# Gathering both experts' token columns in one transposed step, in a mixture-of-experts encoder layer

## The chip, the cores and the metric

The kernel runs on one core of a Trainium2 chip. Times are device microseconds (us) of one execution. The time shown for the kernel before is the median of three runs; one more execution was recorded with a profile, and all rows below come from it. PE is TensorE, DVE is VectorE, ACT is ScalarE, POOL is GpSimd, SP is the engine that issues the transfers (DMA).

## The reference, cut to what matters

One layer of an encoder over 256 tokens of 1024 features: three token mixers (attention, a state-space scan, a convolution), merged and projected, then a normalisation, then a mixture of experts with a second normalisation. What the change touches is the mixture of experts:

```python
logits = (t @ router_w + router_b)
top_vals, top_idx = lax.top_k(logits, 4)            # 4 of 32 experts for each of 256 tokens
gates = softmax(top_vals)
def expert_block(xe, e):                            # xe: the rows of t routed to expert e
    h = xe @ w_gu[e] + b_gu[e]                      # 1024 -> 2048
    gate, up = h[:, :1024], h[:, 1024:]
    gate = minimum(gate, 7.0); up = clip(up, -7.0, 7.0)
    return ((up + 1) * (gate * sigmoid(1.702 * gate))) @ w_dn[e] + b_dn[e]   # 1024 -> 1024
out[token] += gates * expert_block(t[token], e)
x = LN(2**0.25 * x + out)
```

An expert's weights are 12 MB in float32 (8 MB up, 4 MB down), so 32 experts are 384 blocks ("units") of 1 MB.

## The kernel before, in words

The first part of the program (up to L1031) computes the mixers with all weights streamed as 512 KB pieces and split into a rounded part and a remainder, so that each product runs as three products in the format fp32r. While it runs, SP also loads the first units of the experts' weights into a ring of 19 slots of 1 MB (`ring_tile`, L726, and `do_pre`, L732). Unit n uses the slot that unit n-19 had, so from then on SP can issue a load only when PE has used that earlier unit (`load`, L746, in the program's order).

The middle part (L1033 to L1110, a written-out order for all engines) finishes the first normalisation, computes the router's logits, picks the four experts of each token (`choose`), counts for each expert the place of each token (`ranks`), and builds for the first pair of experts a matrix of zeros and ones, `ohp`: one row for each token, one column for each of 64 slots of either expert (`onehot`). `gather_first` multiplies the normalised rows `nrm` (float32, which PE runs as two records for each product) by `ohp`: the result already has the features on the partitions and the slots as columns. `xcopy` applies the scale and shift of the normalisation while it copies PSUM to `xg0`. From `size` the program knows for each expert whether it has up to 32 tokens (0), 33 to 64 (1), or 65 to 96 (2). The rest of the middle part makes what later experts need: `nh_` and `nl_` (the rounded part and the remainder of `nrm`, by ACT at L1093 and by DVE at L939), the gates, and the accumulator `acc`, which POOL writes from `nrm` and the scaled row `lnt` (L1109, L1110).

Then the experts run one after the other (`expert`, L1224), in pairs that share one gather. PE follows the written order; ACT and DVE are ordered by the framework inside a block, and a runtime `If` ends a block. An expert of size 1 runs the arm of 64 columns (`up_many`, tile `pGL`), of size 0 the arm of 32 columns (`up_four`, tile `pGS`), of size 2 both. The 32 columns lie in a tile of their own, `xsm`:

- `small_columns` (L1015) copies the first 32 of the 64 columns with ACT;
- `small_onehot` (L1008) makes their zeros and ones with DVE;
- `If(both > 1)` (L1248) gathers, for an expert of size 2 alone, tokens 65 to 96 into `xsm`: 32 products of 32 columns and 8 copies.

`flush` adds the expert before to `acc`. `fill`, between the up and the down products, gathers for the next pair: in the even expert 8 products of 512 columns give rows of tokens (`gather`, L979), which ACT and DVE copy to `raw`; in the odd expert 8 transposes turn them (`spread_rows`, L994) and 8 copies write `xg`. Then come the down products (L1312 for 64 columns, L1343 for 32), after the transposes of the hidden values (`pTL`, `pTS`) that ACT copies to `hT` (L1306, L1329).

Tiles of the middle part lie in the pool `ch`, which is closed at L1111; the pool `ex` of the experts' temporaries is opened in its place, and each of its tiles waits for the tiles that lay there.

Of the kernel before, what the change touches and what calls it, by code (L numbers as in the profile page):

```python
# [30 lines left out]
TOP = CAP + TINY  # L31
LIMIT = 7.0
# [149 lines left out]
def tile_trunk(ctx, tc, xT_d, xn_d, wf_d, vec_d, row_d, rw_d, cst_d, cst2_d, rope_d, ln1_d, ln2_d,  # L182
# [697 lines left out]
    x1t = [mo.tile([P, KT, P], F32, tag="xg", name=f"x1t{c}", bufs=2) for c in range(2)]  # L880
    raw = mo.tile([P, D], F32, name="rawx")
    xgx = raw.rearrange("p (k n) -> p k n", k=KT)
# [8 lines left out]
    ohp = [mo.tile([P, 2, 2, CAP], F32R, tag="ohp", name=f"ohp{t}", bufs=2) for t in range(1)]  # L891
# [49 lines left out]
    def choose(c):  # L941
        lg = ch.tile([P, NE], F32, name=f"lg{c}")
# [25 lines left out]
    def gates(c):  # L968
        gq = ch.tile([P, 4, NE], F32, tag="gq", name=f"gq{c}", bufs=1)
        V.reciprocal(gs[c][:, 1:2], gs[c][:, 1:2])  # L970
        V.tensor_scalar_mul(ge[c], ge[c], gs[c][:, 1:2])
        V.tensor_tensor(gq, eq[c], ge[c].unsqueeze(2).to_broadcast([P, 4, NE]), op=ALU.mult)
        V.tensor_reduce(Gm[c], gq.rearrange("p k e -> p e k"), axis=AX.X, op=ALU.add)

    def onehot(dst, c, e0):
        V.tensor_tensor(dst[:, c], C("iota_s", 0, CAP).unsqueeze(1).to_broadcast([P, 2, CAP]),
                        rank[c][:, e0:e0 + 2].unsqueeze(2).to_broadcast([P, 2, CAP]), op=ALU.is_equal)

    def gather(pg, c, oh, parts=(0, 1)):  # L979

        for i in parts:
            src = (nh_, nl_)[i]
            for hf in range(2):
                T.matmul(pg[hf], oh, src[:, c, hf * 512:(hf + 1) * 512],
                         start=(c == 0 and i == 0), stop=(c == 1 and i == 1))

    def xcopy(dst, src, k):

        if k >= KT // 2:
# [4 lines left out]
    def spread_rows(dst, src, name):  # L994
        for hf in range(2):
            pT = sm(f"pgt{name}{hf}", [P, 4, P])
            for k in range(4):
                T.transpose(pT[:, k], src(4 * hf + k), C("ident"))
            for k in range(4):
                xcopy(dst[:, 4 * hf + k], pT[:, k], 4 * hf + k)  # L1000

    def gather_first(c):

        for k in range(KT):
            T.matmul(pgd[k // 4][:, k % 4], nrm[c][:, k * P:(k + 1) * P], pair(ohp[0], c).bitcast(F32),
                     start=(c == 0 and k % 4 == 0), stop=(c == 1 and k % 4 == 3))

    def small_onehot(e):  # L1008
        ohs = mo.tile([P, 2, TINY], F32R, tag="ohs", name=f"ohs{e}", bufs=2)
        for c in range(2):  # L1010
            V.tensor_scalar(ohs[:, c], C("iota_s", 0, TINY), base[:, e:e + 1], rank[c][:, e:e + 1],
                            op0=ALU.add, op1=ALU.is_equal)
        return ohs

    def small_columns(e, xg):  # L1015
        lo = (e % 2) * CAP
        xs_ = mo.tile([P, KT, TINY], F32, tag="xsm", name=f"xsm{e}", bufs=1)
        A.copy(xs_, xg[:, :, lo:lo + TINY])  # L1018
        return xs_

    def rowk(k):
        return raw[:, k * P:(k + 1) * P]

    def pair(oh, c):
        return oh[:, c].rearrange("p r s -> p (r s)")
# [5 lines left out]

    PO.memset(rankT.bitcast(F32), 0.0)
    with tc.manual_schedule():  # L1033
# [22 lines left out]
        nrm = [raw, ch.tile([P, D], F32, name="nrm")]  # L1056
# [8 lines left out]
        ranks(0)  # L1065
        zip_run(choose(1), [lambda: None, lambda: V.tensor_mul(rank[0], Pm[0], prk[0]),
# [10 lines left out]
        for c in range(2):  # L1077
# [5 lines left out]
        few = ch.tile([P, NE], F32, name="few")  # L1083
# [12 lines left out]
        for c in range(2):  # L1096
            gates(c)
        cmx = ch.tile([P, 1], F32, name="cmx")
# [117 lines left out]
    def grp(t, g):  # L1216
        return t[g * TINY:(g + 1) * TINY]
# [6 lines left out]
    def expert(e, oh, xg, bl, wt, prev, cur, fill):  # L1224


        pe, da, both = [nc.values_load(size[0:1, e:e + 1], engines=g, min_val=0, max_val=2,
                                       skip_runtime_bounds_check_because="a sum of two comparisons of a count")
                        for g in ((ENG.PE,), (ENG.Activation, ENG.DVE), (ENG.PE, ENG.Activation, ENG.DVE))]
        lo = (e % 2) * CAP  # L1230
        s_ = slice(lo, lo + CAP)
        _, sc, yh, yl = cur

        ohs, xs_ = first if e == 0 else (small_onehot(e), small_columns(e, xg))
        pg = bank(5, f"pgs{e}", [P, KT, TINY])

        def gather_more():
            for k in range(KT):
                for c in range(2):
                    for i, src in enumerate((nh_, nl_)):  # L1240
                        T.matmul(pg[:, k], src[:, c, k * P:(k + 1) * P], ohs[:, c],
                                 start=(c == 0 and i == 0), stop=(c == 1 and i == 1))

        def copy_more():
            for k in range(KT):
                xcopy(xs_[:, k], pg[:, k], k)

        with tc.If(both > 1):  # L1248
            gather_more()
            copy_more()  # L1250
# [13 lines left out]
        def up_four(k0):  # L1264
# [4 lines left out]
            for k in (k0, k0 + 1):  # L1269
                for g, (h, q) in enumerate(QUARTERS):  # L1270
                    T.matmul(grp(pS, g).rearrange("p (g n) -> p g n", g=2), xs_[:, k],  # L1271
                             quarter(wt[k], h, q), start=False, stop=(k == KT - 1))

        for k0 in range(0, KT, 2):
# [82 lines left out]
    def heavy_gather(e, part, ohx):  # L1357
        nm = f"{e}h{part}"
        pg = [sm(f"pgx{nm}{hf}") for hf in range(2)]
        for c in range(2):  # L1360
            gather(pg, c, ohx[:, c])
        rows = []
        for i in range(4):
            r = ex.tile([P, 256], F32, tag=("gv", "uv")[i % 2], name=f"raw{nm}{i}", bufs=2 + i % 2)
            (V.tensor_copy if i % 2 else A.copy)(r, pg[i // 2][:, i % 2 * 256:(i % 2 + 1) * 256])
            rows.append(r)
        spread_rows(xgx, lambda k: rows[k // 2][:, k % 2 * P:(k % 2 + 1) * P], nm)

    def heavy(e, part, wt, cur):
# [3 lines left out]
        heavy_gather(e, part, ohx)  # L1373
# [31 lines left out]
    ENG = mybir.EngineType  # L1405
# [201 lines left out]
```

## Time and profile before

| | us |
|---|---|
| median of three runs (1362.12 to 1366.07) | 1365.44 |
| the profiled execution's own time | 1365.53 |
| its span, first to last instruction | 1363.7 |
| PE busy, share of the span | 1140.3, 84% |
| DVE busy | 559.5, 41% |
| ACT busy | 330.2, 24% |
| moved from memory: 453.27 MB, mean over the span | 333 GB/s |

The span is the profiled execution; 1.83 us lie around it. In the rows, times are from the start of the span. A row of a timeline merges like instructions: start, duration of the merged stretch, engine, line, operation, tiles and shape, count, and in brackets the idle time of that engine before it and what ended it. The letter q behind an engine is its sequencer, which handles branches and semaphores. A float32 product stands as two records, an fp32r product as one; both are printed as f32.

### The profile page before, as it was taken

Reading aid. Unit: us, or ns where it says so; the run is one execution under the profiler, and the core shown is the slowest. Engines: PE = TensorE matmul, PEld = TensorE weight load, DVE = VectorE, ACT = ScalarE, POOL = GpSimd, SP = SyncE. Lnnn points to the kernel's source line nnn. Section 1 sums busy time; section 2 is a strip of 40 time slices with the busy share of each in tenths; the row PEclk is TensorE's granted clock in tenths of the full one; section 3 lists DMA queues with packets and bytes.
Section 4 is the critical chain, followed back from the end, with each engine's and each line's share of the span. In section 5 each row is a group of like instructions: output and inputs, shape, how many; then the busy total and the mean of one; then the engine's idle time right before and its main releaser. Section 6 shows DMA issues by size and latency. Waiting matters only on the chain. (4 is left out here: it accounts for less than half of the span.)

```text
span 1363.7 us, 21824 instructions
## 1 busy us (share of the span) xinstructions
PE 1140.3 (84%) x8035; PEld 595.8 (44%) x8035; DVE 559.5 (41%) x1206; ACT 330.2 (24%) x690; POOL 169.1 (12%) x93
## 2 busy tenths in 40 slices
PE   7999899989978987888888779898888688767875
PEld 6877789889833332322332223232322232212222
DVE  3668888866752323322332222322233222222214
ACT  5666665644421110110010111111111101000101
POOL 3442234457130000000000000000000000000000
PEclk9999899999988999999999899998999999988978
DMA  7334345468879899999999999998999999999991
GB/s 228 124 109 155 124 140 186 155 209 282 313 283 419 344 371 397 418 419 419 417 419 420 419 419 418 420 419 357 387 417 417 419 419 420 418 419 420 418 393 39
DMA packets 73627, 456.47 MB, mean 335 GB/s; under 512 B 8304, under 2 KB 8704, under 8 KB 26752
## 3 DMA queue, kind: packets, MB, share of 16 engines
q1 hardware_dynamic: 73472, 454.35, 83.2%
q8 instruction: 103, 1.69, 0.5%
q14 instruction: 52, 0.43, 0.1%
HBM read 453.27 MB, written 1.05 MB: 333 GB/s over the span
## 5 line engine op out<-in xcount | busy, mean ns | idle before, releaser
L1271 PE MATMUL pGS<-ew,xsm 128*32 128x512 f32 x1408 | 183.8, 627 | 57.4 <-DMA ew<-in_wgu_dram 33.2
L1261 PE MATMUL pGL<-ew,xg 128*64 128x512 f32 x832 | 198.2, 615 | 3.2 <-DMA ew<-in_wgu_dram 2.9
L1205 DVE TENSOR_TENSOR xn<-xn,pos 128x512 f32<-128x512 f32 x124 | 79.8, 684 | 218.1 <-PE pos L1201 218.1
L247 POOL TENSOR_TENSOR wl<-raw,wh 128x1024 fp32r<-128x1024 f32 x56 | 136.8, 2450 | 160.9 <-ACT wh L246 154.6
L1194 DVE SCALAR_TENSOR_TENSOR yl<-pY,gsl,yh 128x512 fp32r<-128x512 f32 x35 | 26.3, 751 | 244.1 <-ACTq L1248 103.3
L1134 ACT ACTIVATE sg<-gv 128x256 f32<-128x256 f32 x48 | 20.0, 417 | 437.5 <-DVE gv L1133 436.7
L1495 POOL TENSOR_TENSOR xn<-xn,lb 128x256 f32<-128x256 f32 x4 | 2.8, 728 | 959.8 <-DVE xn L1483 959.8
L1271 PEld LDWEIGHTS pGS<-ew,xsm 128*32 128x32 f32 x1408 | 44.2, 112 | 156.9 <-issue 93.8
L1343 PE MATMUL pY<-ew,hT 128*32 128x512 f32 x704 | 87.0, 628 | 24.6 <-ACT hT L1329 17.6
L1261 PEld LDWEIGHTS pGL<-ew,xg 128*64 128x64 f32 x832 | 57.4, 140 | 114.3 <-issue 93.5
L246 ACT CAST wh<-raw 128x1024 fp32r<-128x1024 f32 (+1 forms) x89 | 91.1, 1028 | 55.9 <-DMA raw<-in_wf_dram 17.3
L1312 PE MATMUL pY<-ew,hT 128*64 128x512 f32 x416 | 102.2, 648 | 0.0
L1193 ACT ACTIVATE yh<-pY,gsl 128x512 fp32r<-128x512 f32 x35 | 24.1, 687 | 197.0 <-PEq L1316 71.4
L247 DVE TENSOR_TENSOR wl<-raw,wh 128x1024 fp32r<-128x1024 f32 (+1 forms) x33 | 41.5, 1263 | 41.9 <-ACT wh L246 41.9
L1312 PEld LDWEIGHTS pY<-ew,hT 128*64 128x64 f32 x416 | 31.0, 149 | 61.9 <-issue 60.4
L1343 PEld LDWEIGHTS pY<-ew,hT 128*32 128x32 f32 x704 | 20.4, 114 | 75.6 <-issue 33.6
L1267 PE MATMUL pGS<-bgu_t,bl 128*32 128x512 f32 x176 | 26.3, 664 | 28.7 <-DVEq L1248 10.9
L1018 ACT COPY xsm<-xg 128x256 f32<-128x256 f32 x32 | 12.9, 402 | 148.4 <-PE pGS L1271 132.0
L1201 PEld LDWEIGHTS pos<-yh,sc 64*128 64x128 f32 x124 | 12.2, 183 | 56.9 <-issue 56.9
L1325 PE MATMUL pY<-bdn_t,bl 128*32 128x512 f32 x88 | 24.0, 623 | 14.3 <-PEq L1316 14.3
L1201 PE MATMUL pos<-yh,sc 64*128 64x512 f32 x124 | 31.0, 491 | 4.7 <-PEq L1277 4.7
L417 DVE SCALAR_TENSOR_TENSOR xacc<-xp,vec,xacc 128x256 f32<-128x256 f32 x48 | 32.4, 676 | 2.7 <-ACT xacc L415 1.5
(462 smaller groups left out, 2126.2 us busy)
## 6 DMA issues: line engine op xcount, KB each, us to landing
ew<-in_wgu_dram SPq DMA_DIRECT2D x241, 1024.0 KB, 19.9
ew<-in_wdn_dram SPq DMA_DIRECT2D x124, 1024.0 KB, 19.9
raw<-in_wf_dram SPq DMA_DIRECT2D x87, 512.0 KB, 3.6
ew<-in_wgu_dram SPq DMA_DIRECT2D x30, 512.0 KB, 6.3
ew<-in_wdn_dram SPq DMA_DIRECT2D x8, 512.0 KB, 4.6
xraw<-in_xT_dram SPq DMA_DIRECT2D x4, 256.0 KB, 5.8
xn<-in_xn_dram SPq DMA_DIRECT2D x2, 512.0 KB, 5.3
lnt<-in_ln_dram SPq DMA_DIRECT2D x2, 512.0 KB, 10.5
```

The costliest lines, as they stand in the source:

```text
L246: A.copy(h[:, b], raw[:, b])
L247: (PO if u in LOW_POOL else V).tensor_sub(l[:, b], raw[:, b], h[:, b].bitcast(F32))
L417: V.scalar_tensor_tensor(acc, xp[:, j:j + S], W("cw5", t * 5 + j), acc, op0=ALU.mult, op1=ALU.add)
L1193: A.activation(yh, pY, AF.Copy, scale=gsl)
L1194: V.scalar_tensor_tensor(yl, pY, gsl, yh.bitcast(F32), op0=ALU.mult, op1=ALU.subtract)
L1201: T.matmul(pos[n], sc[r, c * P:(c + 1) * P], y[r], start=(start and i == 0), stop=(i == 1))
L1205: V.tensor_add(dst, dst, po)
L1261: T.matmul(pL[q][h * 64:(h + 1) * 64].rearrange("p (g n) -> p g n", g=2), xg[:, k, s_], quarter(wt[k], h, q), start=False, stop=(k == KT - 1))
L1267: T.matmul(grp(pS, g), bl[:, g * TINY:(g + 1) * TINY].bitcast(F32), bgu_t[:, q * 512:(q + 1) * 512].bitcast(F32), start=True, stop=False)
L1271: T.matmul(grp(pS, g).rearrange("p (g n) -> p g n", g=2), xs_[:, k], quarter(wt[k], h, q), start=False, stop=(k == KT - 1))
L1312: T.matmul(pY[0][n * 64:(n + 1) * 64], hT[b][:, j, h * CAP:(h + 1) * CAP], wt[KT + 2 * b + h][:, j, n * 512:(n + 1) * 512], start=False, s ...
L1343: T.matmul(grp(pY, 2 * n + j), hT[:, j, g * TINY:(g + 1) * TINY], w[:, j, n * 512:(n + 1) * 512], start=(j == 1 and (b, h) == (0, 0)), sto ...
```

## The change

The two kinds of columns become one matrix. For a pair of experts `ohp` now has 192 columns: 64 and 64, then 32 and 32. `xg` holds 192 columns likewise, and `xsm`, `raw` and the copy L1018 are gone.

- `gather` now multiplies 128 features of `nh_` or `nl_` (the stationary operand) by the 192 columns of `ohp`: 4 products for each of 8 blocks of features. The even expert's `fill` gathers blocks 0 to 3, the odd expert's 4 to 7, each with four copies, two by ACT and two by DVE. The transposes are gone.
- For an expert of size 2 the 32 columns hold tokens 65 to 96, else the first 32 (through `base`), so the `If` of L1248 stands only for experts 0 and 1, whose small columns are still copied from the wide ones.
- In the middle part the first transpose of `prt` and a first half of the counts `pn` come ahead of the gather, the first gather runs by halves, the halves are copied by one engine each, and the small columns, the `If` and its register loads for expert 0 come ahead of the second transpose of `prt`, `rankT`, `nh_`, `lnt` and the gates. `nrm` has both its tiles in `ch`.

```diff
+SL = 2 * TOP
-    raw = mo.tile([P, D], F32, name="rawx")
-    ohp = [mo.tile([P, 2, 2, CAP], F32R, tag="ohp", name=f"ohp{t}", bufs=2) for t in range(1)]
+    ohp = [mo.tile([P, 2, SL], F32R, tag="ohp", name="ohp0", bufs=2)]
...
+    def onehot_small(dst, c, e):
+        V.tensor_scalar(small(dst, c, e), C("iota_s", 0, TINY), base[:, e:e + 1], rank[c][:, e:e + 1],
+                        op0=ALU.add, op1=ALU.is_equal)
+    def gather(dst, oh, k0, name):
+        n = oh.shape[-1]
+        pt = sm(f"pgx{name}{k0}", [P, 2, n])
+        for k in (k0, k0 + 1):
+            for c in range(2):
+                for i, src in enumerate((nh_, nl_)):
+                    T.matmul(pt[:, k - k0], src[:, c, k * P:(k + 1) * P], oh[:, c],
+                             start=(c == 0 and i == 0), stop=(c == 1 and i == 1))
+        for k in (k0, k0 + 1):
+            xcopy(dst(k), pt[:, k - k0], k, k // 2 % 2)
...
+    def more_columns(e, both, pg, rows):
+        with tc.If(both > 1):
+            ...
+            for k in range(KT):
+                xcopy(small(xg0, k, e), pg[:, k], k)
...
-        nrm = [raw, ch.tile([P, D], F32, name="nrm")]
+        nrm = [ch.tile([P, D], F32, name=f"nrm{c}") for c in range(2)]
...
         ranks(0)
+        pn = mm("pn", [P, NE])
+        T.matmul(pn, C("ones"), Pm[0], start=True, stop=False)
...
-        gather_first(0)
         T.transpose(prt[:, 0], rank[0], C("ident"))
+        gather_first(0, 0)
         ranks(1)
         V.tensor_mul(rank[1], Pm[1], prk[1])
         onehot(ohp[0], 1, 0)
-        pn = mm("pn", [P, NE])
-        for c in range(2):
-            T.matmul(pn, C("ones"), Pm[c], start=(c == 0), stop=(c == 1))
-        T.transpose(prt[:, 1], rank[1], C("ident"))
-        gather_first(1)
-        A.copy(rankT[0:NE], prt.rearrange("e c t -> e (c t)"))
+        T.matmul(pn, C("ones"), Pm[1], start=False, stop=True)
+        gather_first(0, 1)
...
+        for hf in range(2):
+            gather_first(1, hf)
+            for k in range(4):
+                xcopy(xg0[:, 4 * hf + k, 0:P], pgd[hf][:, k], 4 * hf + k, hf)
+        for e in range(2):
+            A.copy(xg0[:, :, P + e * TINY:P + (e + 1) * TINY], xg0[:, :, e * CAP:e * CAP + TINY])
+            if e == 0:
+                first = sizes(0)
+                more_columns(0, first[2], mm("pgs0", [P, KT, TINY]), (nrm,))
+        T.transpose(prt[:, 1], rank[1], C("ident"))
+        A.copy(rankT[0:NE], prt.rearrange("e c t -> e (c t)"))
...
-        ohs, xs_ = first if e == 0 else (small_onehot(e), small_columns(e, xg))
-        with tc.If(both > 1):
-            gather_more()
-            copy_more()
+        if e == 1:
+            more_columns(e, both, bank(5, f"pgs{e}", [P, KT, TINY]), ...)
...
-                    T.matmul(grp(pS, g).rearrange("p (g n) -> p g n", g=2), xs_[:, k],
+                    T.matmul(grp(pS, g).rearrange("p (g n) -> p g n", g=2), xg[:, k, x_],
...
                     for c in range(2):
                         onehot(ohn, c, e + 2)
+                        for i in range(2):
+                            onehot_small(ohn, c, e + 2 + i)
...
+        def fill(e=e, more=more):
+            if more:
+                for k0 in (0, 2) if e % 2 == 0 else (4, 6):
+                    gather(lambda k: xgn[:, k], ohn, k0, str(e))
```

The path for experts with more than 96 tokens uses the new `gather` too; with these inputs it is skipped.

## Rows read from the trace of the kernel before

**Rows 1.** Page, the span in 40 slices: busy tenths of the DMA engines.
```profile
DMA  7334345468879899999999999998999999999991
```
**Rows 2.** Windows: stretch, length, busy (count) by engine, clock, DMA share, GB/s.
```profile
378.00:394.00 16.00, 10.26 (x68) 4.40 (x72) 13.41 (x32) 6.07 (x10) 8.06 (x6) 0.85 0.35 133
469.00:481.00 12.00, 9.88 (x63) 3.13 (x60) 3.69 (x6) 1.61 (x3) 0.00 (x0) 1.00 0.35 132
509.00:515.00 6.00, 3.27 (x22) 0.93 (x22) 0.98 (x2) 0.69 (x1) 0.00 (x0) 1.00 0.43 147
514.00:930.00 416.00, 347.98 (x2312) 124.97 (x2306) 119.37 (x290) 48.37 (x114) 0.00 (x0) 0.95 1.01 419
930.00:942.00 12.00, 9.80 (x63) 2.98 (x59) 3.69 (x6) 1.42 (x3) 0.00 (x0) 1.00 0.60 237
970.00:974.00 4.00, 1.50 (x10) 0.37 (x10) 0.78 (x2) 0.69 (x1) 0.00 (x0) 0.93 0.44 127
```
**Rows 3.** Timeline of PE: the last wait for weights ahead of the late stops.
```profile
811.32 1.06 PE L1343 MATMUL pY<-ew,hT 128*32 128x512 f32 x8 [1.17 <-DMA ew<-in_wdn_dram]
```
**Rows 4.** Timeline of PE: last wait for weights, and the last expert's start.
```profile
1286.45 1.94 PE L1261 MATMUL pGL<-ew,xg 128*64 128x512 f32 x8 [0.29 <-DMA ew<-in_wgu_dram]
1312.68 1.19 PE L1257 MATMUL pGL<-bgu_t,bl 128*128 128x512 f32 x2 [6.95 <-DVEq L1444]
```
**Rows 5.** Timeline of PE: first and last of expert 2's 32 conditional products.
```profile
432.40 0.28 PE L1241 MATMUL pgs<-ohs,nh 128*128 128x32 f32 x1
435.88 0.26 PE L1241 MATMUL pgs<-ohs,nl 128*128 128x32 f32 x1
```
**Rows 6.** Windows, columns as above: a stretch of mixer products of 256 columns.
```profile
320.00:340.00 20.00, 20.00 (x171) 20.00 (x171) 14.11 (x21) 9.82 (x13) 13.74 (x6) 1.00 0.86 302
```
**Rows 7.** Timeline of PE: an even expert's gather, to its down products.
```profile
461.48 0.73 PE L984 MATMUL pgx<-nh,ohp 128*128 128x512 f32 x2
463.45 0.40 PE L1302 MATMUL pY<-bdn_t,bl 128*128 128x512 f32 x1
464.99 7.09 PE L1312 MATMUL pY<-ew,hT 128*64 128x512 f32 x32
```
**Rows 8.** Timeline of PE: experts 3 and 15, from their transposes to down products.
```profile
499.12 1.06 PE L998 MATMUL pgt<-cst,rawx 128*128 128x128 f32 x8
503.96 7.09 PE L1312 MATMUL pY<-ew,hT 128*64 128x512 f32 x32
...
843.31 1.09 PE L998 MATMUL pgt<-cst,rawx 128*128 128x128 f32 x8
848.32 9.86 PE L1312 MATMUL pY<-ew,hT 128*64 128x512 f32 x32
```
**Rows 9.** Timeline, all engines: first gather to first expert's transposes.
```profile
378.39 2.47 PE L1005 MATMUL pgd<-ohp,nrm 128*128 128x128 f32 x16
382.37 0.40 ACT L1018 COPY xsm<-xg 128x256 f32<-128x256 f32 x1 [0.85 <-DVE gs L970]
386.67 3.42 PE L1271 MATMUL pGS<-ew,xsm 128*32 128x512 f32 x16 [3.88 <-ACTq L1248]
391.11 2.37 DVE L976 TENSOR_TENSOR ohp<-cst,rank 128x128 fp32r<-128x128 f32 x2
395.99 1.27 POOL L1110 TENSOR_TENSOR xn<-xn,lnt 128x512 f32<-128x512 f32 x1
396.01 1.50 DVE L1011 TENSOR_SCALAR ohs<-cst,base,rank 128x32 fp32r<-128x32 f32 x2 [2.53 <-PE aux L1144]
402.24 0.51 PE L1328 MATMUL pTS<-cst,uv 128*128 128x128 f32 x2
```
**Rows 10.** Timeline of PE: expert 1, from its transposes to its down products.
```profile
419.91 0.66 PE L998 MATMUL pgt<-cst,rawx 128*128 128x128 f32 x4
427.05 5.41 PE L1343 MATMUL pY<-ew,hT 128*32 128x512 f32 x32 [0.53 <-ACT hT L1329]
```
**Rows 11.** Timeline of PE: start of expert 3, past the untaken branch of L1248.
```profile
480.70 0.70 PE L1257 MATMUL pGL<-bgu_t,bl 128*128 128x512 f32 x2 [0.45 <-PEq L1248]
```

More of the change, by code (lines that the diff above doesn't have):

```diff
@@ L879, in tile_trunk @@
     acc = xn
[L880 to L882 removed]
+    x1t = [mo.tile([P, KT, SL], F32, tag="xg", name=f"x1t{c}", bufs=2)[:, :, 0:P] for c in range(2)]
     blt = mo.tile([P, NE, 2], F32R, name="blt")
@@ L992, in xcopy @@
             A.activation(dst, src, AF.Identity, scale=lgb[:, 0, k:k + 1], bias=lgb[:, 1, k:k + 1])
[L994 to L1006, printed above, removed]
@@ L1021, in rowk, with gather_first, sizes @@
[L1021 to L1025, printed above, removed]
+    def gather_first(c, hf):
+        for k in range(4):
+            kk = 4 * hf + k
+            T.matmul(pgd[hf][:, k], nrm[c][:, kk * P:(kk + 1) * P], ohp[0][:, c, 0:P].bitcast(F32),
+                     start=(c == 0 and k == 0), stop=(c == 1 and k == 3))
+    def sizes(e):
+        return [nc.values_load(size[0:1, e:e + 1], engines=g, min_val=0, max_val=2,
+                               skip_runtime_bounds_check_because="a sum of two comparisons of a count")
+                for g in ((ENG.PE,), (ENG.Activation, ENG.DVE), (ENG.PE, ENG.Activation, ENG.DVE))]
@@ new lines, in more_columns @@
+    def more_columns(e, both, pg, rows):
+        with tc.If(both > 1):
+            for k in range(KT):
+                for c in range(2):
+                    for i, src in enumerate(rows):
+                        oh = small(ohp[0], c, e)
+                        l = src[c][:, k * P:(k + 1) * P]
+                        T.matmul(pg[:, k], l, oh.bitcast(F32) if len(rows) == 1 else oh,
+                                 start=(c == 0 and i == 0), stop=(c == 1 and i == len(rows) - 1))
+            for k in range(KT):
+                xcopy(small(xg0, k, e), pg[:, k], k)
@@ L1097, in tile_trunk @@
             gates(c)
+        for c in range(2):
+            onehot_small(ohp[0], c, 1)
         cmx = ch.tile([P, 1], F32, name="cmx")
@@ L1224, in expert @@
     def expert(e, oh, xg, bl, wt, prev, cur, fill):
-        pe, da, both = [nc.values_load(size[0:1, e:e + 1], engines=g, min_val=0, max_val=2,
-                                       skip_runtime_bounds_check_because="a sum of two comparisons of a count")
-                        for g in ((ENG.PE,), (ENG.Activation, ENG.DVE), (ENG.PE, ENG.Activation, ENG.DVE))]
+        pe, da, both = first if e == 0 else sizes(e)
         lo = (e % 2) * CAP
         s_ = slice(lo, lo + CAP)
+        x_ = slice(P + (e % 2) * TINY, P + (e % 2 + 1) * TINY)
         _, sc, yh, yl = cur
-        ohs, xs_ = first if e == 0 else (small_onehot(e), small_columns(e, xg))
[L1235 to L1246, printed above, removed]
-        with tc.If(both > 1):
-            gather_more()
-            copy_more()
+        if e == 1:
+            more_columns(e, both, bank(5, f"pgs{e}", [P, KT, TINY]), ([nh_[:, c] for c in range(2)], [nl_[:, c] for c in range(2)]))
         pL = [bank(2 + q, f"pGL{e}{q}") for q in range(2)]
@@ L1358, in heavy_gather @@
         nm = f"{e}h{part}"
[L1359 to L1367, printed above, removed]
+        rows = [ex.tile([P, 2, P], F32, tag=("gv", "uv")[i % 2], name=f"xgx{nm}{i}", bufs=2 + i % 2) for i in range(4)]
+        for k0 in range(0, KT, 2):
+            gather(lambda k: rows[k // 2][:, k % 2], ohx, k0, nm)
+        return rows
     def heavy(e, part, wt, cur):
```

66 lines of the change are left out of this document (22 added, 44 removed).

## The prediction

> **What bounds the kernel now.** I read the page's slices first. From the tenth slice on the transfers are nearly always busy [rows 1]: 384 units of 1 MB must come in, and in a stretch without a stop they come at 419 GB/s [rows 2], which is 2.50 us each. So I asked where the transfers stop, with windows over the places where the rate dips. A window's loss is its length times (419 - rate) / 419: 10.9 us in 378 to 394, 8.2 in 469 to 481, 3.9 in 509 to 515, 5.2 in 930 to 942, 2.8 in 970 to 974 [rows 2]. Together 31.0 us: that much, and no more, can be won ahead of the tail by an earlier PE, because a stop is a full ring that waits for PE to use a unit.
>
> Then PE's timeline, to see where PE waits for weights and where weights wait for PE. From the start of expert 0 to the start of expert 4 (386 to 514) PE waits for no transfer: its chain alone sets when the stop at 509 ends. From 514 to 930 the transfers don't stop. PE waits for them for the last time at 811.32 [rows 3]; from there through expert 19's start (974) PE is the later one again, and its chain sets the end of the last two stops. After that the transfers run through, PE waits for one at 1286.45 [rows 4], and from there the last two experts and the closing normalisation hang on PE. So the end moves by three sums: PE's chain of 386 to 514, its chain of 811 to 974 (at most the 5.2 + 2.8 = 8.0 us of its stops), and the tail.
>
> **The change part by part.**
>
> The price of one new product decides all. A product has 128 features loaded and 192 columns moved. The trace has none with 192. With 32 columns, 32 of them take from 432.40 to 435.88, or 0.112 us each [rows 5]; in a stretch of mostly 256 columns 171 take 20 us, or 0.117 each [rows 6]. 192 lies between; I take 0.115. A fill has 16: 1.84 us. It replaces 8 wide products in even experts, 461.48 to 463.45, or 1.97 [rows 7] (+0.1 us of gain), and 8 transposes of 1.06 [rows 8] in odd ones. The far upper bound is a full float32 product: 8 of 128 columns (16 records) take 2.47 us [rows 9], 0.309 each, which by columns is 0.46 for 192. The far lower one is 0.112.
>
> On this the Trainium skill has a rule that speaks against the change: "TensorE: Matmul & The Clock Gate", Part 3, "The mechanism", says that a weight load overlaps a running product only where the two use different row groups, and these all use the full 128 rows. By that rule load and product add up. The trace disagrees at 256 columns, where load and product together take 0.117 us [rows 6]; what it would give for 192 is the third rival below.
>
> Start of expert 0. PE idles until 386.67, although its columns are ready at 382.77 (382.37 + 0.40): in ACT's order the `If` of L1248 stands behind the casts of `nh_` and the scaling of `lnt`, and PE waits for ACT to pass it [rows 9]. The change puts the `If` ahead of these, and about 0.7 us of transposes and counts (0.5 of `pn`, 0.2 of `prt`) ahead of or out of the gather; PE should start near 382. Of these 4.7 us I don't count all, for what is late next is DVE and POOL. Expert 0's gather needs the zeros and ones of the next pair, which DVE makes behind `nl_`: 2.37 us for two wide ones while POOL is running, and 1.50 for two small ones [rows 9], of which there are now four. From about 390.3 (0.8 us earlier than now, by the shorter list ahead) that is 2.37 + 3.0, so 395.7; the gather follows, 1.84, then 0.8 of branches and 1.0 of bias products as now, so the transposes stand at 399.4 instead of 402.24: a gain of 2.8. Also, `gv` and the other temporaries now lie where `lnt` lay, which POOL reads until 397.26 [rows 9]; DVE can write `gv` only then, and `uv` 1.9 us later, 399.2. Queued on DVE behind that wait are only expert 0's own steps, and PE's transposes wait for them. So both limits lie near 399.3. PE idles some 3 us ahead of the gather and may fall to 1.2 GHz, as it has here for its first 16 records: 3.42 us [rows 9] against 1.92 for the same step of later experts. I take 2.0, bounds 0.5 and 3.4.
>
> Expert 1. From its transposes to its down products 7.14 us [rows 10]; the wait is DVE's, which frees a PSUM bank late, and the clock falls behind it. Without the wait it would be as expert 4, a small one, 4.9 (525.93 to 530.82). If the bank still comes at 422.5, the new gather ends 0.2 later than the transposes; if not, 2.2 are won and 1.8 more on the 32 down records at full clock (5.41 against 3.64). I take 1.5, bounds -0.2 and 4.0.
>
> Expert 2 is of size 2: its 32 conditional products go, 432.40 to 435.99, and 0.1 of gather: 3.7 [rows 5]. Their replacement is already in the fills.
>
> Expert 3. From the transposes to the down products 4.84 [rows 8], for ACT and DVE work through eight copies and `xsm` before ACT comes to `hT`. An even expert with four lighter copies needs 3.51 for the same stretch [rows 7], with 1.84 of gather 3.4: gain 1.4. An untaken L1248 costs PE 0.45 at an expert's start [rows 11]; gone at experts 3 and 4: 0.9.
>
> First sum: 2.0 + 1.5 + 3.7 + 1.4 + 0.9 = 9.5, bounds 6.3 and 13.5. The two early stops (12.1) and the head's (10.9) hold that.
>
> Second sum, 811 to 974: experts 15 and 17 are of size 2 as well, 3.6 each, 7.2; their odd fills shrink from 5.0 [rows 8] and 4.9 to 3.4, 3.1; the branch goes five times less the two that are taken, 1.35; experts 16 and 18 win 0.1 each. 11.8 us, and up to 5.5 more if the clock no longer falls behind the long `hT` waits (9.86 for 32 down records in expert 15, 7.09 in expert 3 [rows 8]; expert 17 is like 15). That is more than the stops hold, so 8.0, with 3.8 to spare.
>
> Tail: experts 30 and 31 gather nothing. One untaken branch less and no `xsm` ahead of expert 31's 6.95 us of idling [rows 4]: 0.5, bounds 0 and 1. Everywhere else transfers cover PE: more columns for DVE to compare, fewer and smaller copies, all beside them.
>
> Sum: 9.5 + 8.0 + 0.5 = 18.0. Against the profiled execution, 1365.53 (span 1363.7 and 1.83 around it; the median is 0.1 lower), that gives 1347.5, and with all bounds 1343.0 to 1351.2.
>
> **The rivals.**
>
> 1. The head's gain is swallowed: expert 0 stands behind POOL and DVE, PE falls to 1.2 GHz, and expert 1 keeps its bank wait. For it: both limits at 399.3. Against: PE's up products are done earlier all the same. First sum 0.5 - 0.2 + 3.7 + 1.4 + 0.9 = 6.3, tail 0: 1351.2; with a further 1 to 2 lost in expert 0 to a slow clock, 1353.
>
> 2. Slower: the 192-column products run at float32's pace. For it: no row has an fp32r product between 32 and 256 columns, and at 32 the load (0.112) may hide a slow product. Against: 0.117 at 256. At four times the wide product's 0.246 (1.97 / 8 [rows 7]) cut to 192 of 512 columns, 0.37, or 0.255 over my price: the first chain has 56 of them, -14.3, the second 64, 11.8 - 16.3. The end moves by 9.5 - 14.3 - 4.5 + 0.5 = -8.8: 1374. It decides from 0.30 us a product (120 products, 21.8 us of gain to eat).
>
> 3. Load and product add up: 0.112 + 192 x 0.246 / 512 = 0.20 each. Then 56 x 0.085 = 4.8 go from the first sum, and the second is 11.8 - 5.4 = 6.4: 1353.9.
>
> 4. The change doesn't move the stops, because they come from something else than PE's chain (SP's own order): only the start's 2.0 and the tail's 0.5 remain: 1363.0.
>
> **How the numbers follow.** Forecast 0.62, rival 1 0.15, rival 3 0.06, rival 2 0.11, rival 4 0.06. A measurement of this kernel tells 0.3% (4.1 us) from no change, 1361.3 to 1369.5. Forecast, rivals 1 and 3 are faster: 0.83; rival 4, and a mild rival 2, the same: 0.07; the rest slower: 0.10. Likeliest 1347.5, its own range 1343 to 1352. The range: 1341, for clock gains not counted, to 1361, which leaves out rival 2 and most of rival 4.
>
> **What would show it.** Right: 16 narrow products in about 1.85 us in each fill; the first up product near 382 and expert 0's transposes near 399.4; no wait over 1 us for `hT` in odd experts; expert 4 starting some 9 us earlier; no loss of transfers between 900 and 980. Wrong: narrow products over 0.2 us each, a stop that stays in 930 to 974, or new waits of PE behind DVE in expert 0.

## The result and the profile after

The changed kernel takes 1354.11 us (median of five runs, 1351.92 to 1356.15) against 1366.07 for the kernel before beside it (five runs, 1362.12 to 1368.19): ratio 0.9913, interval 0.9892 to 0.9934. The gain of the medians is 12.0 us, 0.9%, clear of the noise; the forecast, 1347.5, had 18.0. The profiled execution took 1351.92 with a span of 1350.1, 13.6 less than the span before; rival 1 had given 1351.2 to 1353.

First the page's slices of the changed kernel (busy tenths of the transfer engines, and the granted clock), which answer to [rows 1], and windows, which answer to [rows 2] (stretch, length, busy time and count by engine, clock, transfer share, GB/s).

```profile
PEclk9999899999988999999989889999998999998988
DMA  6434345467889899999999999999999999999981
```
```profile
376.00:392.00 16.00, 13.23 (x114) 7.14 (x117) 12.20 (x33) 6.38 (x11) 5.11 (x4) 0.89 0.64 233
462.00:478.00 16.00, 14.18 (x82) 4.58 (x80) 4.18 (x7) 1.76 (x3) 0.00 (x0) 1.00 0.50 190
500.00:512.00 12.00, 9.27 (x59) 2.90 (x59) 1.95 (x4) 0.69 (x1) 0.00 (x0) 1.00 0.91 350
515.00:900.00 385.00, 329.32 (x2280) 120.98 (x2273) 109.58 (x266) 37.52 (x80) 0.00 (x0) 0.97 1.01 419
930.00:942.00 12.00, 11.14 (x82) 5.66 (x80) 4.26 (x12) 2.52 (x6) 0.00 (x0) 1.00 1.01 419
970.00:974.00 4.00, 3.54 (x40) 0.94 (x28) 0.88 (x2) 0.69 (x1) 0.00 (x0) 1.00 1.01 416
```

Lost by the prediction's formula: 16 x (419 - 233) / 419 = 7.1, then 8.7 and 2.0; nothing after 515. The two late stops are gone. Of 31.0 us of stops 17.8 are left. The difference, 13.2, is close to the 13.6 of the span, but not all of the 13.6 comes from stops: 11.6 of it stand ahead of PE's last wait for weights (1286.45 in [rows 4], 1274.83 below) and 2.0 behind it.

To compare pieces of PE's chain I take one yardstick in every trace: the router's second maximum on DVE, the last event that all kernels share ahead of the change, and the start of expert 4. Two fences, the kernel before and the changed one, from the timeline:

```profile
372.75 0.19 DVE L949 MAX8 v<-lg 128x8 f32<-128x32 f32 x1
...
407.73 1.07 PE L1267 MATMUL pGS<-bgu_t,bl 128*32 128x512 f32 x8 [0.87 <-PEq L1275]
...
513.78 1.07 PE L1267 MATMUL pGS<-bgu_t,bl 128*32 128x512 f32 x8 [2.73 <-DVEq L1248]
```
```profile
372.56 0.19 DVE L948 MAX8 v<-lg 128x8 f32<-128x32 f32 x1
...
381.21 1.25 PE L1268 MATMUL pGS<-bgu_t,bl 128*32 128x512 f32 x8 [0.32 <-PEq L1276]
383.12 1.92 PE L1272 MATMUL pGS<-ew,xg 128*32 128x512 f32 x16 [0.66 <-ACTq L1024]
392.43 1.46 DVE L982 TENSOR_SCALAR ohp<-cst,base,rank 128x32 fp32r<-128x32 f32 x2
393.26 0.35 PE L998 MATMUL pgx<-ohp,nh 128*128 128x192 f32 x1
396.33 1.26 POOL L1128 TENSOR_TENSOR xn<-xn,lnt 128x512 f32<-128x512 f32 x1
397.63 0.42 DVE L1151 TENSOR_SCALAR gv<-pGS 128x256 f32<-128x256 f32 x1 [3.75 <-POOL xn L1128]
399.63 0.47 PE L1329 MATMUL pTS<-cst,uv 128*128 128x128 f32 x2 [1.97 <-DVEq L1301]
400.72 5.00 PE L1344 MATMUL pY<-ew,hT 128*32 128x512 f32 x32 [0.62 <-ACT hT L1330]
406.61 1.06 PE L1268 MATMUL pGS<-bgu_t,bl 128*32 128x512 f32 x8 [0.88 <-PEq L1276]
421.73 0.36 PE L998 MATMUL pgx<-ohp,nh 128*128 128x192 f32 x1 [1.52 <-DVE xn L1223]
426.41 5.81 PE L1344 MATMUL pY<-ew,hT 128*32 128x512 f32 x32 [0.62 <-ACT hT L1330]
432.15 0.73 PE L1258 MATMUL pGL<-bgu_t,bl 128*128 128x512 f32 x2
...
507.55 1.06 PE L1268 MATMUL pGS<-bgu_t,bl 128*32 128x512 f32 x8 [2.17 <-DVEq L1323]
```

From the second maximum to the first up product PE wins 3.4 us (13.92 to 10.56; [rows 9] has the former), to expert 0's transposes 2.4 (29.49 to 27.07), to expert 1's start only 0.9 (34.98 to 34.05). `gv` starts at 397.63, right when POOL has read `lnt` for the last time (396.33 + 1.26); PE idles 1.97 for it, and the 32 down records behind take 5.00 instead of 3.64. The other limit that the prediction had for expert 0, the zeros and ones beside POOL, does not bind: the last of them are done at 393.89, where 395.7 was predicted. In expert 1 the second half of the gather waits 1.52 for DVE's late addition into `acc`, and its down records take 5.81 (5.41 before, [rows 10]). From expert 2's start to expert 4 it is 81.38 before (513.78 - 432.40, [rows 5]) and 75.40 after, 6.0 less.

A fill's price, from expert 2's: the first of 16 narrow products and what follows the last.

```profile
457.65 0.35 PE L998 MATMUL pgx<-ohp,nh 128*128 128x192 f32 x1
...
459.52 0.42 PE L1303 MATMUL pY<-bdn_t,bl 128*128 128x512 f32 x1
```

1.87 us for 16, 0.117 each, and 0.111 from one to the next: no more than for 32 columns (0.112, [rows 5]), so load and product do not add up. The Trainium skill ("TensorE: Matmul & The Clock Gate", Part 3, "The mechanism") says in one place that a load overlaps a running product only in other row groups, though the same section also speaks of a background weight buffer. The trace decides against the first: here loads of all 128 rows hide behind products of 192 columns.

The late part: expert 15, where PE idled 2.82 for `hT` and its 32 down records took 9.86 ([rows 8]), first the kernel before, then the changed one; then the last wait for weights and expert 31's start, which answer to [rows 4], with expert 30's down records between them, and last the same records of the kernel before.

```profile
847.68 0.70 PE L1305 MATMUL pTL<-cst,uv 128*128 128x128 f32 x2 [2.82 <-ACT hT L1306]
```
```profile
836.82 0.50 PE L1306 MATMUL pTL<-cst,uv 128*128 128x128 f32 x2 [0.56 <-ACT hT L1307]
837.25 7.09 PE L1313 MATMUL pY<-ew,hT 128*64 128x512 f32 x32
...
1274.83 1.94 PE L1262 MATMUL pGL<-ew,xg 128*64 128x512 f32 x8 [0.29 <-DMA ew<-in_wgu_dram]
1285.16 7.09 PE L1313 MATMUL pY<-ew,hT 128*64 128x512 f32 x32
1299.02 1.19 PE L1258 MATMUL pGL<-bgu_t,bl 128*128 128x512 f32 x2 [6.78 <-DVEq L1436]
```
```profile
1296.94 8.78 PE L1312 MATMUL pY<-ew,hT 128*64 128x512 f32 x32
```

In expert 15 the wait is now 0.56 and the records take 7.09. The wait ahead of expert 31 is still there, 6.78 for 6.95. From expert 4's start to the last wait for weights it is 772.67 before and 767.28 after, 5.4 less; from there to the end of the span 77.25 and 75.27, 2.0 less, of which 1.7 are expert 30's down records (8.78 and 7.09).

### The profile page after: what moved, and what is told of

Its sections match the earlier page's. It is cut to its first block, busy times and chain, and to the rows that moved or that the text cites. A ratio compares the mean times of both kernels' runs of the same rounds, so it can differ in the third digit from the quotient of the medians.

```text
span 1350.1 us, 21768 instructions
## 1 busy us (share of the span) xinstructions
PE 1139.7 (84%) x8179; PEld 604.0 (45%) x8179; DVE 545.5 (40%) x1179; ACT 312.1 (23%) x633; POOL 168.5 (12%) x93
## 5 line engine op out<-in xcount | busy, mean ns | idle before, releaser
L1272 PE MATMUL pGS<-ew,xg 128*32 128x512 f32 x1408 | 191.2, 641 | 67.8 <-DMA ew<-in_wgu_dram 50.3
L1272 PEld LDWEIGHTS pGS<-ew,xg 128*32 128x32 f32 x1408 | 42.3, 112 | 171.9 <-DMA ew<-in_wgu_dram 70.8
L1313 PE MATMUL pY<-ew,hT 128*64 128x512 f32 x416 | 92.1, 595 | 0.0
L998 PE MATMUL pgx<-ohp,nh 128*128 128x192 f32 x240 | 62.6, 300 | 3.0 <-DVE xn L1223 1.5
L998 PEld LDWEIGHTS pgx<-ohp,nh 128*128 128x128 f32 x240 | 49.7, 207 | 34.5 <-issue 19.7
L998 PE MATMUL pgx<-ohp,nl 128*128 128x192 f32 x240 | 59.5, 287 | 0.0
L998 PEld LDWEIGHTS pgx<-ohp,nl 128*128 128x128 f32 x240 | 49.5, 206 | 0.0
L1288 DVE COPY gsl<-aux 128x2 f32<-128x2 f32 x32 | 5.1, 159 | 107.1 <-PE aux L1162 58.9
L1268 PE MATMUL pGS<-bgu_t,bl 128*32 128x512 f32 x176 | 24.8, 625 | 20.6 <-DVEq L1323 13.2
```

Source lines behind the costliest of these rows:

```text
L998: T.matmul(pt[:, k - k0], src[:, c, k * P:(k + 1) * P], oh[:, c], start=(c == 0 and i == 0), stop=(c == 1 and i == 1))
L1268: T.matmul(grp(pS, g), bl[:, g * TINY:(g + 1) * TINY].bitcast(F32), bgu_t[:, q * 512:(q + 1) * 512].bitcast(F32), start=True, stop=False)
L1272: T.matmul(grp(pS, g).rearrange("p (g n) -> p g n", g=2), xg[:, k, x_], quarter(wt[k], h, q), start=False, stop=(k == KT - 1))
L1313: T.matmul(pY[0][n * 64:(n + 1) * 64], hT[b][:, j, h * CAP:(h + 1) * CAP], wt[KT + 2 * b + h][:, j, n * 512:(n + 1) * 512], start=False, s ...
```

## The experiments

Every kernel is the changed one with the edit shown. The table cuts each trace with the yardstick: e0 from the second maximum to expert 1's start, e1 to expert 2's start, e2+3 to expert 4's start, rest to the end of the span. Ratios are to the kernel before on the same chip. They were taken in three groups, each beside its own runs of the kernel before: the three with "thrice" and cond_early; overlay, bank1, both and head_back; ordered, best, back_ordered and late_four. The changed kernel stands in none of them, so a difference from its 0.9913 is less sure than one inside a group. The pieces come from one profiled execution each.

| kernel | ratio (interval) | e0 | e1 | e2+3 | sum | rest |
|---|---|---|---|---|---|---|
| before | 1 | 34.98 | 24.67 | 81.38 | 141.03 | 849.9 |
| changed | 0.9913 (0.9892 to 0.9934) | 34.05 | 25.54 | 75.40 | 134.99 | 842.6 |
| early_thrice | 0.9957 (0.9939 to 0.9976) | 35.01 | 26.78 | 86.56 | 148.35 | 842.0 |
| mid_thrice | 0.9885 (0.9852 to 0.9918) | 34.07 | 22.69 | 75.41 | 132.17 | 840.3 |
| late_thrice | 0.9884 (0.9856 to 0.9912) | 33.91 | 25.57 | 75.41 | 134.89 | 839.4 |
| cond_early | 0.9947 (0.9923 to 0.9971) | 34.14 | 25.54 | 79.73 | 139.41 | 845.8 |
| overlay | 0.9927 (0.9902 to 0.9952) | 38.42 | 22.44 | 75.35 | 136.21 | 843.6 |
| bank1 | 0.9874 (0.9844 to 0.9904) | 35.13 | 20.92 | 75.40 | 131.45 | 845.4 |
| both | 0.9931 (0.9904 to 0.9958) | 39.55 | 20.67 | 75.43 | 135.65 | 843.9 |
| head_back | 0.9961 (0.9938 to 0.9984) | 40.48 | 25.47 | 75.59 | 141.54 | 845.8 |
| ordered | 0.9875 (0.9840 to 0.9909) | 30.83 | 25.14 | 75.24 | 131.21 | 842.2 |
| best | 0.9859 (0.9826 to 0.9892) | 31.61 | 20.79 | 75.14 | 127.54 | 843.8 |
| back_ordered | 0.9898 (0.9862 to 0.9933) | 32.49 | 25.16 | 75.42 | 133.07 | 845.1 |
| late_four | 0.9940 (0.9917 to 0.9963) | 33.75 | 22.69 | 75.41 | 131.85 | 849.9 |

**Does the time follow the first chain? The same added work in three places, and the conditional gather put back.**

```diff
-        for k in (k0, k0 + 1):
+        for k in [k for _ in range(times) for k in (k0, k0 + 1)]:
...
-                    gather(lambda k: xgn[:, k], ohn, k0, str(e))
+                    gather(lambda k: xgn[:, k], ohn, k0, str(e), 3 if e in (2, 3) else 1)
```

early_thrice, `e in (2, 3)`:

> The changed kernel, with the 16 narrow gather products in the fills of experts 2 and 3 issued three times into the same PSUM tile (the result is the same): 64 more products on PE, 64 x 0.115 = 7.4 us, and nothing else. My theory (the time follows PE's chain from the start of the experts to expert 4, because stops of the transfers at 462 to 478 and 500 to 512 wait for it): all of it shows, expert 4 starts 7.4 us later, at about 515, the stops grow by as much, and the time is 1354.1 + 7.4 = 1361.5. Rival A (PE work anywhere costs its time): the same 7.4 here, but also in the same edit elsewhere. Rival B (what the change won came from the second chain, experts 15 to 19, and the first is covered): 1354.

mid_thrice, `e in (6, 7)`:

> The same 64 more products, 7.4 us of PE, in the fills of experts 6 and 7, where the transfers run without a stop. My theory: PE waits for weights there anyway, nothing moves, 1354.1 (within 2 us). Rival A (PE work anywhere costs its time): 1361.5.

late_thrice, `e in (15, 16)`:

> The same 64 more products, 7.4 us of PE, in the fills of experts 15 and 16, inside the second chain (811 to 974 of the kernel before), whose stops of 8.0 us are gone. My theory: the chain was made 11.8 us shorter than it was, 8.0 of which the stops could give back, so 3.8 are spare and the rest of the 7.4 shows: at most 1354.1 + 3.6 = 1357.7, with a small stop near 930 to 974 again; if the clock that no longer falls there added to the spare, 1354. Rival A, and rival B (no spare): 1361.5.

The same 7.4 us of PE cost time at experts 2 and 3 and nothing at 6 and 7 or 15 and 16: 0.44% (6.0 us) against the changed kernel, 0.72% (9.8 us) against mid_thrice beside it. In early_thrice's own trace e2+3 is 11.2 longer: 7.1 of products (5.4 instead of 1.9 in either fill), 1.0 of a wait for the fill's copies, and the rest is mostly clock, granted 0.50 (1.2 GHz) from 480 to 486, where expert 2's last 32 down records take 5.34 instead of 3.64. The stop moves behind 512 (windows of early_thrice, columns as above):

```profile
500.00:512.00 12.00, 11.69 (x99) 7.68 (x96) 4.73 (x16) 1.75 (x4) 0.00 (x0) 1.00 1.02 423
512.00:530.00 18.00, 14.57 (x80) 4.97 (x82) 3.03 (x6) 1.45 (x3) 0.00 (x0) 0.91 0.72 285
```

Rivals A and B fall. That late_thrice cost no time that shows says that more than 3.8 us are spare there. Its windows have two small stops again, 0.4 and 0.6 us, so the 7.4 are about what it can take:

```profile
920.00:930.00 10.00, 8.23 (x54) 2.71 (x54) 4.23 (x7) 1.76 (x3) 0.00 (x0) 1.00 1.00 403
950.00:960.00 10.00, 7.85 (x42) 2.61 (x45) 1.17 (x3) 1.07 (x2) 0.00 (x0) 1.00 0.97 392
```

cond_early puts `more_columns` back at experts 2 and 3:

```diff
-        if e == 1:
+        if e == 1 or e in (2, 3):
             more_columns(e, both, bank(5, ...), ..., oh, xg)
```

> The changed kernel with the conditional gather of the 32 further columns put back at the start of experts 2 and 3 alone (it writes the same values as are there already): taken in expert 2, not taken in expert 3. My theory: 32 products, 3.6 us, and about 0.45 us for each branch, so expert 4 starts 4.0 to 4.5 us later and the time is 1358.1 to 1358.6. Rival B (the first chain is covered): 1354.

e2+3 grows by 4.33, as expected. The ratio grows by 0.34% (4.6 us) against the changed kernel, but there the intervals overlap; it is clear of mid_thrice and late_thrice, beside which it was timed (0.6%, 8.5 us). That it costs time is shown, how much only by the trace.

late_four, `e in (15, 16, 17, 18)`:

> The changed kernel with the fills of experts 15 to 18 issued three times: 128 more products, 14.7 us of PE in the second chain (the 7.4 in experts 15 and 16 alone didn't show). My theory: 3.8 spare by the count of instructions and up to 5.5 by the clock, 9.3 in all, so at least 5.4 show, as a stop of the transfers in 930 to 980, and at most 10.9: ratio 0.995 to 0.999. Rival G (there is no second chain any more, PE is far ahead): nothing, 0.989 to 0.991.

The rest grows from 842.6 to 849.9, by 7.3, and the stops are back (windows of late_four: 2.6, 2.4 and 4.9 lost):

```profile
900.00:930.00 30.00, 26.90 (x176) 12.76 (x172) 10.78 (x28) 4.00 (x9) 0.00 (x0) 0.90 0.93 383
930.00:950.00 20.00, 19.37 (x119) 6.46 (x113) 3.61 (x7) 0.69 (x1) 0.00 (x0) 0.97 0.94 368
950.00:980.00 30.00, 25.60 (x184) 12.11 (x184) 8.32 (x21) 3.21 (x7) 0.00 (x0) 0.94 0.85 350
```

So the second chain is still a limit, 5 to 7 us behind: 14.7 less the 9.9 of stops, or less the 7.3 of the rest (the rest of other kernels varies by 6 us, 839.4 to 845.8). late_thrice agrees: 7.4 less its 1.0 of stops. The ratio, 0.9940, lies a little below the expected range, and its interval overlaps that of the changed kernel; that rival G falls rests on the stops in the trace.

**Why experts 0 and 1 gave so little.** Expert 1 first: its second gather half in a free bank.

```diff
-        pt = sm(f"pgx{name}{k0}", [P, 2, n])
+        pt = pt or sm(f"pgx{name}{k0}", [P, 2, n])
...
+    bank(0, ...) if (e, k0) == (1, 6) else None
```

bank1:

> The changed kernel with the second half of expert 1's gather in a PSUM bank that is free (that of the down products of 64 columns), instead of one that waits for DVE's late sum into acc. Taken away: PE's wait of 1.52 us ahead of this half. My theory: the 1.5 come off, and where the clock no longer falls behind the wait the 32 down records take 3.64 instead of 5.81 and the transposes and bias products 0.7 less, so 1.5 to 4.4 off: ratio 0.988 to 0.990; from the second maximum to expert 4's start 130.6 to 133.5. Rival D (the wait is covered by what DVE does next): the transposes wait for DVE instead, 0.991.

e1 is 20.92 instead of 25.54: 1.5 of wait, 2.2 of clock in the down records, and most of the remainder clock in the bias products and transposes ahead of them. The sum is inside the expected, the ratio slightly below. (The profiled execution of bank1 took 1359.90, 10.6 above its median; 8.6 of that stand ahead of the second maximum, where the code is the changed kernel's.) In the timeline of bank1, expert 1's down records are at full clock, as also in both and best:

```profile
433.69 3.64 PE L1344 MATMUL pY<-ew,hT 128*32 128x512 f32 x32 [0.62 <-ACT hT L1330]
```

With the wait left in, mid_thrice, late_four and overlay have 3.64 here too; the changed kernel, late_thrice, cond_early and early_thrice have 5.73 to 5.87, and head_back, ordered and back_ordered, further down, 4.92 to 5.66. Windows of PE over the transposes and the first of these records, first of the changed kernel, then of mid_thrice (length, PE busy, clock, transfer share, GB/s):

```profile
424.00:428.00 4.00, 3.38 (x14) 0.50 1.01 410
```
```profile
428.00:432.00 4.00, 3.38 (x30) 1.00 1.02 414
```

A granted clock of 0.50 is 1.2 GHz, 1.00 is 2.4. Behind this wait it is down in some executions and not in others, and that makes e1 25.5 or 22.7. So 1.5 to 1.8 of bank1's 4.6 are sure, and the rest is won only against executions in which the clock falls.

Then expert 0: the temporaries off what POOL reads.

```diff
-        lnt = ch.tile([P, 2, D], F32, name="lnt")
         nrm = [ch.tile([P, D], F32, name=f"nrm{c}") for c in range(2)]
+        lnt = ch.tile([P, 2, D], F32, name="lnt")
...
+        for c, h in halves: PO.tensor_tensor(acc[:, c, h], nrm[c][:, h], lnt[:, 0, h], op=ALU.mult)
+        for c, h in halves: PO.tensor_tensor(acc[:, c, h], acc[:, c, h], lnt[:, 1, h], op=ALU.add)
...
+    first_uv = [gate_tiles(f"0_{q}") for q in range(3)]
     parked = (ex.tile([P, S], F32R, name="sc"), ...
```

overlay:

> The changed kernel with expert 0's temporaries no longer over the scaled row that POOL reads: the normalised rows lie ahead of lnt, the temporaries of the swiglu are taken first, and POOL does its four products before its four sums. Taken away: DVE's wait for POOL ahead of gv (3.75 us), behind which PE idles 1.97 ahead of expert 0's transposes and then runs the 32 down records at a lower clock (5.00 us, 3.64 at full clock; 6.2 in other runs of the same code). My theory (expert 0 stands behind POOL, and the first chain sets the end): PE's idling of 1.97 goes and the 32 records take 3.64, so 3.3 us (up to 4.6) come off: ratio to the kernel before 0.9913 - 0.0024 = 0.989, and from the router's second maximum to expert 4's start 131.7 instead of 135.0. Rival C (expert 0 stands behind something else, DVE's zeros and ones beside POOL): nothing moves, 0.991.

both:

> Both edits. My theory: both add up, 4.8 to 9.0 us off, the stops of the transfers at 462 to 512 (10.7 us in the changed kernel) shrink by as much: ratio 0.985 to 0.988, from the second maximum to expert 4's start 126.0 to 130.2. If the first chain is covered by then (stops gone, or weights late): less than the sum of the two.

Overlay and both miss. e0 became 4.4 and 5.5 longer, not 3.3 shorter; in both this eats what expert 1 gains. DVE's and PE's timelines of overlay show why:

```profile
393.36 1.10 DVE L976 TENSOR_TENSOR ohp<-cst,rank 128x128 fp32r<-128x128 f32 x1
398.00 0.42 DVE L1151 TENSOR_SCALAR gv<-pGS 128x256 f32<-128x256 f32 x1 [3.54 <-PE pGS L1272]
400.88 1.44 DVE L982 TENSOR_SCALAR ohp<-cst,base,rank 128x32 fp32r<-128x32 f32 x2
402.46 0.50 PE L998 MATMUL pgx<-ohp,nh 128*128 128x192 f32 x1 [4.53 <-DVE ohp L982]
```

`gv` no longer waits for POOL, but the framework has now put the swiglu ahead of the remaining zeros and ones. DVE stands 3.54 for the end of the up products with work behind it that PE's gather needs, and the gather waits 4.53. In the changed kernel all zeros and ones are ahead of `gv`.

head_back undoes the moved block:

```diff
-        for e in range(2):                # ahead of T.transpose(prt[:, 1], ...)
-            A.copy(xg0[:, :, P + e * TINY:...], ...)
-            if e == 0: first = sizes(0); more_columns(0, ...)
+        # the same lines, behind gates(c)
```

> The changed kernel with the first expert's block (small columns, the If and its register loads) put back behind rankT, nh, the scaling of lnt and the gates, as in the kernel before; nothing else is undone. The first up product comes 3.5 us later (at about 386.7 instead of 383.1). My theory (expert 0's end stands behind POOL, not behind PE's start): PE's idling of 1.97 ahead of the transposes goes, the transposes stand 1.6 later, and the clock is full behind them (3.64 instead of 5.00), so 0.2 us net, -1.2 to +1.6: ratio 0.990 to 0.9925. Rival E (moving the block up brings what PE's start shows): 3.5 us slower, ratio 0.9939.

Worse than either: e0 40.48, 6.4 more. DVE's and PE's timelines of head_back have the same turned order, and a slow `nl_` beside POOL:

```profile
389.24 6.18 DVE L938 TENSOR_TENSOR nl<-nrm,nh 128x512 fp32r<-128x512 f32 x4
400.21 0.42 DVE L1151 TENSOR_SCALAR gv<-pGS 128x256 f32<-128x256 f32 x1 [3.50 <-PE pGS L1272]
401.99 0.50 DVE L982 TENSOR_SCALAR ohp<-cst,base,rank 128x32 fp32r<-128x32 f32 x2
402.63 0.43 PE L998 MATMUL pgx<-ohp,nh 128*128 128x192 f32 x1 [2.65 <-DVE ohp L982]
```

So the next three write DVE's order out: the zeros and ones of the second pair ahead of `nl_`.

```diff
+        pair1 = (mo.tile(..., name="ohp2"), mo.tile(..., name="xg2"))
+        for c in range(2):
+            onehot(pair1[0], c, 2)
+            for i in range(2): onehot_small(pair1[0], c, 2 + i)
         for c in range(2):
             for n in range(2): low(c, n, V)
```

ordered (with the overlay's edit):

> The first overlay kernel, in which the gather of expert 0's fill waited 4.53 us for the small zeros and ones that DVE had behind the swiglu, with one more edit: the zeros and ones of the second pair are written out in the middle part, ahead of nl, so that DVE makes them before POOL starts and nothing of expert 0 stands ahead of them. My theory (two things follow one another here: POOL's hold on the temporaries, and DVE's order, which the framework turned round when the first was taken away): now PE's idling of 1.97 ahead of the transposes goes, no new wait takes its place, the 32 down records take 3.64 instead of 5.0 to 6.3; from the second maximum to expert 4's start 130.4 to 133.0 (135.0 in the changed kernel, 136.2 with the overlay alone), ratio 0.9885 to 0.990. Rival F (DVE beside POOL is slow whatever the order): as the overlay alone, 136 and 0.9927.

best (ordered and bank1):

> The same with expert 1's second gather half in the free bank too. My theory: 126.8 to 129.5 from the second maximum to expert 4's start (131.45 with the free bank alone, less the 1.97 and 2.7 of clock), ratio 0.984 to 0.987. If the first chain has become short enough for something else to set the end: no better than the free bank alone, 0.9874.

back_ordered (on head_back):

> The kernel with the first expert's block put back (141.5 from the second maximum to expert 4's start, ratio 0.9961), with the zeros and ones of the second pair written out ahead of nl. In the former PE started 3.4 us later and its gather then waited 2.65 for DVE's small zeros and ones, again behind the swiglu. My theory: the 2.65 go, and up to 2.1 of slow clock with them; 3.4 stay, which belong to the block itself: 136.7 to 138.9, ratio 0.992 to 0.994. Rival (the block's own place costs all of the 6.5): 141.5, 0.996.

In ordered e0 is 30.83, 3.2 less than in the changed kernel; sum and ratio are as expected (the ratio a little lower), and rival F falls. The expectation missed one thing: a new wait did take the place, 1.70 for `hT`, which ACT can write only when POOL is done (the row shows the wait; that the tile now lies over `lnt` is inferred). And the full clock behind this wait is not sure: in best the same records took 5.34 behind 1.67. PE and ACT of ordered (lines 6 higher from here on):

```profile
397.92 0.50 PE L1335 MATMUL pTS<-cst,uv 128*128 128x128 f32 x2
400.12 3.64 PE L1350 MATMUL pY<-ew,hT 128*32 128x512 f32 x32 [1.70 <-ACT hT L1336]
```
```profile
399.68 0.38 ACT L1336 ACTIVATE hT<-pTS 128x256 f32<-128x256 f32 x1 [3.48 <-POOL xn L1134]
```

best has 127.54, inside the expected, and ratio 0.9859 (median 1346.17, 1343.94 to 1347.67): it beats the kernel before clearly; from the changed kernel, timed beside other runs, it stands 0.5% away with intervals that touch at 0.9892.

back_ordered misses on the other side: 133.07, no worse than the changed kernel, where I had expected 3.4 more. Its PE and DVE timelines:

```profile
386.58 1.28 PE L1274 MATMUL pGS<-bgu_t,bl 128*32 128x512 f32 x8 [0.73 <-DVE xg L1006]
390.80 3.37 PE L1278 MATMUL pGS<-ew,xg 128*32 128x512 f32 x16 [2.94 <-ACTq L1024]
406.14 0.51 PE L1335 MATMUL pTS<-cst,uv 128*128 128x128 f32 x2
407.28 3.64 PE L1350 MATMUL pY<-ew,hT 128*32 128x512 f32 x32 [0.63 <-ACT hT L1336]
```
```profile
402.69 0.42 DVE L1157 TENSOR_SCALAR gv<-pGS 128x256 f32<-128x256 f32 x1 [0.50 <-PE pGS L1278]
```

PE starts later, the first step runs slowly, and still the transposes stand 26.84 behind the second maximum, against 27.07. A part of this does not come from the edit: the first gather's 24 records ahead took 3.56 instead of 4.81, so expert 0's first bias product stands 1.4 earlier. Counted from that product (386.58, and 381.21 in the changed kernel) the transposes come 1.1 later; but PE comes when POOL is done, without idling, and the clock is full behind it, which takes 1.4 back. The zeros and ones run beside POOL here and are as slow as in overlay (1.45 for two small ones), and nothing waits for them: here their order counts, not their pace. With DVE's order held, the place of the block is worth nothing that these runs show. They don't separate it fully: ordered, 1.9 shorter, also has the overlay's edit, and the changed kernel with nothing but the order written out was not run. What made the framework turn the order was not tried.

## Why the prediction was right or wrong

- **What bounds the kernel: right, its sizes less so.** Two chains and the stops. The late stops held 8.0 and are gone, but from expert 4's start to the last wait for weights only 5.4 came off (772.67 to 767.28, and 767.1 to 767.3 in the six other traces whose last wait is this one); where the other 2.6 went is open. The tail gave 2.0 instead of 0.5, 1.7 of it by expert 30's clock, which the prediction had not counted: luck that hid most of this. That 3.8, and with the clock perhaps 9.3, were to spare came out as 5 to 7.
- **Price of a narrow product: right**, 0.111 to 0.117 for 0.115. Rivals 2 (0.30 and more) and 3 (0.20) fall. Rival 3's time, 1353.9, is the nearest of all to the median, by chance: its price is refuted. Rival 4 falls by early_thrice and by the late stops, which are gone. (The first chain has 64 new products, four fills of 16, not 56, so rival 3 would give 1354.5 and rival 2 1376; and the upper bound of the first sum is 13.4, not 13.5.)
- **Experts 2 and 3: right.** 3.7 + 1.4 + 0.9 = 6.0 predicted, 5.98 measured, and e2+3 is the same within 0.05 in the six other traces with this code.
- **Expert 0: the step that failed first.** Its transposes came as predicted (2.4 earlier for 2.8, with `gv` behind POOL as said), but I kept 2.0 at expert 1's start and 0.9 came (-0.2 to 1.2 in the seven traces with this code): PE still idled 1.97, and the clock that I had put down as a possible loss fell in all seven (4.95 to 6.33 for 32 records, where 3.64 is full). That is a new wait behind DVE in expert 0, which the prediction itself had listed as a sign of being wrong.
- **Expert 1: the step that failed most.** I took 1.5 on the chance that the bank comes free earlier. It doesn't: DVE still makes its last addition behind expert 1's swiglu. With the slow clock behind the wait the profile shows -0.9, with the full clock of mid_thrice and late_four +2.0. The former lies outside my lower bound of -0.2, which had kept the wait but not counted 0.4 more for the down records (5.81 for 5.41) and 0.3 ahead of the gather.
- **The forecast against rival 1.** Rival 1 said exactly this (POOL and DVE, slow clock, the bank wait kept), and its first sum, 6.3, is what the profile has, 6.0. I gave it 0.15 because PE's up products end earlier; they do, and then wait. 18.0 predicted, less 3.5 in the first sum and 1.2 in the two others, is the 13.4 of the table (sum and rest); the second maximum stood 0.2 earlier. The median lies 6.6 above the forecast, above the likeliest stretch (1343 to 1352) and within the wide range. That it lies in this range is in part luck: the range was drawn for clock gains and for a part of rival 4, not for a first sum below its lower bound.
- **The rest of the distance is spread.** Kernels with the same first chain and no added cost gave 0.9913, 0.9885 and 0.9884. In the profiles the second maximum itself, ahead of everything changed, lies between 372.6 and 381.2, and expert 0's first product follows it by 7.2 to 8.8.

## What to carry over

When a move makes an engine start earlier, follow each resource that the next step needs (here the memory under a tile, and a bank) up to the next meeting point, and count only what is left there. An edit that frees one wait can make the framework put the waiting instruction earlier in an in-order queue: look at what then stands behind it, and write that order out. Before pricing work on an engine that is busy 84% of the time, ask in which stretch it sets the end: the same 7.4 us cost 6 to 10 in one place and nothing in two.

## Not expected of the hardware

- DVE and POOL slow each other. Two small comparisons (128 x 32) take 0.50 us alone and 1.45 beside POOL's operations; `nl_`'s four take 2.49 (ordered), 3.58 (changed), and 6.18 where POOL runs beside all of them (head_back); POOL's single operations take 1.26 where DVE waits and up to 1.73 beside `nl_`.
- The same 32 records of expert 1 behind the same 1.52 us of idling run in 3.64 or in some 5.8 us, in executions of code that is the same up to there. Without the idling they took 3.64 in all three traces. Expert 0's did the same behind about 1.7 us: 3.64 in ordered, 5.34 in best. What decides it stays open.
- Why the second maximum moves by up to 8.6 us between executions of the same code ahead of it was not looked into.
